# One MoE kernel on one core: the two experts of a pair in alternate blocks, and other start addresses for TensorE's stationary operands

## The chip, the cores and the metric

The kernel runs on one NeuronCore of a Trainium2 chip. The metric is the device time of one execution in microseconds, taken as the median over several runs. Lower is better. The profile is one further execution of the same program, recorded by the hardware profiler.

## The reference

The reference is a decoder of two blocks with 256 tokens and a model width of 1024, all in float32. The first block is two layers of mixer and feed-forward; its second feed-forward is the mixture of experts that this case is about:

```python
def moe_swiglu(h, router, w_gate, w_up, w_down):
    t = h.reshape(-1, d)                                  # 256 x 1024
    logits = (t @ router).astype(jnp.float32)
    top_v, top_i = lax.top_k(logits, TOP_K)               # TOP_K = 2 of N_EXPERTS = 8
    top_w = jax.nn.softmax(top_v, axis=-1)
    gates = jnp.sum(jax.nn.one_hot(top_i, N_EXPERTS) * top_w[..., None], axis=1)
    for e in range(N_EXPERTS):
        y_e = swiglu(t, w_gate[e], w_up[e], w_down[e])    # 1024 -> 3584 -> 1024
        out = out + gates[:, e:e + 1] * y_e
```

The second block (two layers of feed-forward, a mixer of convolutions and gating, feed-forward) follows; nothing in it is changed.

## The kernel before

**Precision.** TensorE takes float32 operands rounded to a shorter form (fp32r in the rows). To keep float32 accuracy each operand is split into a high and a low half, and a product is made of three matmuls: high x high, high x low, low x high (`mm3t`, lines 339 to 344 and their matmuls L341 to L343). Weights stream from HBM and are split on the way: a DMA brings 1 MB into one of four buffers `raw` (`load`, L297, on SP's queue), ScalarE (ACT) writes `hi` by a cast (L318), VectorE (DVE) writes `lo = raw - hi` (L319). One `hi` and one `lo` tile hold 128 x 1024 values, half a load; I call that a **part**. There are five `hi` and five `lo` buffers.

**The MoE** (`moe`, line 1059, and `moe_pass`, line 1219) works expert by expert. The experts are put into an order by their token counts: `ORDER` gives each of the eight positions a rank of size, and the positions whose rank is in `FEW = (1, 2, 3)`, the second of each of the first three pairs, are expected to hold at most `SMALL = 64` tokens. Such a **few** expert packs the high halves of its 64 tokens and the low halves of the same 64 into the 128 columns of one stationary operand, so it needs two matmuls (L1293, L1294) where a **full** expert (at most 128 tokens) needs three. It streams as many weights as a full one. A routing that doesn't fit the sizes goes through an extra pass under `tc.If` (L1205), which the inputs here don't take.

Two positions make a pair. `prep(p)` (line 1228) gathers the tokens of both experts of a pair by a selection matrix into `xeh` and `xel` (in every second pair into the model's own `xh` and `xl`), and makes the gates `gs` and the matrix `PT` that puts results back. Then, for each expert, the loop at line 1311 runs over seven blocks of 512 hidden columns:

1. gate and up: 8 parts, 4 for each of two PSUM banks, with the tokens (`xeh`) as the stationary operand and the weights moving;
2. SiLU and product into `mh` (full: L1330 on ACT, L1331 on DVE; few: two copies `mh` and `mu`, L1328 on ACT);
3. `down(*prev)` for the block before: 4 parts, stationary operand `mhh` (and `mhl`), into two PSUM banks `acc` that gather over all seven blocks;
4. transposes of `mh` (full L1352, few L1342 and then L1345, L1346), and the split into `mhh` and `mhl` (L478, L479).

So an expert has 84 parts. At its end `acc` is scaled and split into `yh`, `yl` (L1361, L1362), and `back()` multiplies by `PT` (16 matmuls, L1369, L1370) and adds to the model's state `X` (L401); it is called inside the first block of the next expert.

**PSUM.** All eight banks are taken: four buffers `bank` for gate and up, two `side0` and two `side1` for the rest (`acc`, the transposes, `prep`, `back`).

**Order of the work.** A scheduler places the instructions of each engine in a fixed queue, from its own estimate of when each is ready; every engine then works through its queue in order. Weight loads and splits are put ahead by `tc.high_priority`.

**Addresses.** Pools lay tiles one after the other. `SHIFT` pads the tile `Pf` (line 1230) and so moves the tiles behind it in their pool; lines 29 to 37 hold such constants. In the program before, the stationary tiles of a partition begin at these byte addresses modulo 512: `xeh`, `xel` at 288, `mhh`, `mhl` at 96, `xh`, `xl` in the MoE at 128.

Of the kernel before, what the change touches and what calls it, by code (L numbers as in the profile page):

```python
# [27 lines left out]
SMALL = 64  # L28
# [5 lines left out]
PHASE = {"h": 64, "l": 320}  # L34
STILL = 128
BASE = 128
SHIFT = 40

# [182 lines left out]
class Builder:  # L221
# [837 lines left out]
    def moe(self, gain):  # L1059
        nc, tc = self.nc, self.tc  # L1060
        p0 = self.par0
        with tc.tile_pool(name="moe", bufs=1) as pl, tc.tile_pool(name="moew", bufs=2) as wk:
            f = lambda n, name: pl.tile([128] + list(n), F32, name=name)

            early = {}
            self.expert = [0]
            with tc.high_priority(offset=AHEAD):
                for i in range(PRE):
                    early[0, i] = self.load(*self.moe_load(0, i))
                for (e, i), tags, pool, bufs in EARLY:  # L1070
                    ap, kt, n = self.moe_load(e, i)
# [14 lines left out]
            nc.gpsimd.tensor_scalar(key, p0("iota")[:, 0:8], 1.0 / 16, None, op0=ALU.mult)  # L1086
            nc.gpsimd.memset(key[:, 0:1], -1000.0)

            iotas = f([2, SMALL], "iotas")
            nc.gpsimd.tensor_copy(iotas, p0("iota")[:, 0:SMALL].rearrange("p (o n) -> p o n", o=1)  # L1090
                                  .to_broadcast([128, 2, SMALL]))
            ident2 = f([SMALL], "ident2")
# [8 lines left out]
            bt = self.side()  # L1101
# [19 lines left out]
            mm = nc.tensor.matmul  # L1121
# [62 lines left out]
            ci, ei = f([2, 8], "ci"), f([2, 8], "ei")  # L1184
# [12 lines left out]
            args = (pl, wk, xnh, xnl, posq, G, iotas, ident2)  # L1197
            nxt = self.moe_pass(args, False, 0, 1, None, early, more=True)

            early = {(2, i): self.weights(*self.moe_load(2, i)) for i in range(SPL)}  # L1200
            with tc.high_priority(offset=AHEAD):
                for i in range(SPL, SPL + PRE):
                    early[2, i] = self.load(*self.moe_load(2, i))
# [15 lines left out]
    def moe_pass(self, args, off, p0, p1, gain, early, cur=None, more=False):  # L1219

        nc = self.nc
        pl, wk, xnh, xnl, pos, G, iotas, ident2 = args
        mm = nc.tensor.matmul
# [1 line left out]
        ot = pl if off else wk  # L1225
        few = lambda e: ORDER[e] in FEW and not off

        def prep(p):

            Pf = wk.tile([128, 512 + SHIFT], F32, name="Pf", bufs=1)[:, :512] \  # L1230
                .rearrange("p (m a n) -> p m a n", m=2, a=2)
            Pr = wk.tile([128, 2, 256], F32R, name="Pr", bufs=1)
            for m in range(2):
                for a in range(2):
                    nc.vector.tensor_scalar(Pf[:, m, a], iotas.rearrange("p a n -> p (a n)") if few(2 * p + a) else iota,
                                            pos[:, m, 2 * p + a:2 * p + a + 1], None, op0=ALU.is_equal)
            nc.scalar.copy(Pr, Pf.rearrange("p m a n -> p m (a n)"))
            if p % 2 and not off:
                xeh, xel = self.xh, self.xl
            else:  # L1240
                xeh, xel = (pl.tile([128, KD, 256], F32R, name=n) for n in ("xeh", "xel"))
            for k in range(0, KD, 2):
                for src, dst, eng in ((xnh, xeh, nc.scalar.copy), (xnl, xel, nc.vector.tensor_copy)):
                    b = self.side()
                    for i in range(2):
                        for m in range(2):
                            mm(b[:, i * 256:(i + 1) * 256], src[:, m, (k + i) * 128:(k + i + 1) * 128], Pr[:, m],
                               start=(i == 0 and m == 0), stop=(i == 1 and m == 1), skip_group_check=True)
# [8 lines left out]
            bg = self.side()  # L1257
            for a in range(2):
                for m in range(2):
                    mm(bg[:, a * 9:(a + 1) * 9], Pf[:, m, a], G[:, m], start=(a == 0 and m == 0),  # L1260
                       stop=(a == 1 and m == 1), skip_group_check=True)
            gs = ot.tile([128, 2, 2], F32, name="gs")
            for a in range(2):
                e = 2 * p + a
                nc.vector.tensor_copy(gs[:, a, 0:1], bg[:, a * 9 + e:a * 9 + e + 1])
                nc.vector.tensor_copy(gs[:, a, 1:2], bg[:, a * 9 + 8:a * 9 + 9])
            bt = self.side()
            for a in range(2):
                for m in range(2):
                    nc.tensor.transpose(bt[:, a * 256 + m * 128:a * 256 + (m + 1) * 128], Pf[:, m, a], self.ident)  # L1270
            PT = ot.tile([128, 2, 256], F32R, name="PT")
            nc.scalar.copy(PT.rearrange("p a t -> p (a t)"), bt)
            return PT, gs, xeh, xel

        nxt, back = None, None
        for e in range(2 * p0, 2 * p1):
            a = e % 2
            if cur is None:
                if back:
                    back()  # L1280
                    back = None
                cur = prep(e // 2)
# [12 lines left out]

            def down(f0, hh, hl):
                if not acc:
                    acc.extend(self.side() for _ in range(2))
                for k0 in (0, 2):
                    wt = self.weights(wd.block(f0 + k0 * 128, 2, 0, D), 2, D)  # L1300
                    for k in range(2):
                        for n in range(2):
                            mms(acc[n], hh[:, k0 + k], None if hl is None else hl[:, k0 + k],
                                *wt(k, n * 512, (n + 1) * 512),
                                start=(f0 + k0 + k == 0), stop=(f0 + (k0 + k + 1) * 128 == 3584))

            prev = None
            for ci in range(7):
                b2 = []
                for wi in range(2):  # L1310
                    b = self.bank()
                    for ki in range(2):
                        i = ci * 4 + wi * 2 + ki
                        pre = early.get((e, i))
                        wt = pre if callable(pre) else self.weights(*self.moe_load(e, i), pre)
                        for k in range(4):
                            k0 = ki * 4 + k
# [14 lines left out]
                if ci == 6 and a == 1 and not off and (e + 1 < 2 * p1 or more):  # L1332
                    nxt = prep(e // 2 + 1)
                if prev:
                    down(*prev)
                bt = self.side()
                hh = wk.tile([128, 4, 128], F32R, name="mhh")
                if few(e):
                    n = 4 * SMALL
# [10 lines left out]
                else:  # L1350
# [5 lines left out]
                prev = (ci * 512, hh, hl)  # L1356
            down(*prev)
            yh, yl = wk.tile([128, D], F32R, name="yh", bufs=1), wk.tile([128, D], F32R, name="yl", bufs=1)
            for n in range(2):
                ns = slice(n * 512, (n + 1) * 512)  # L1360
                nc.scalar.activation(yh[:, ns], acc[n], AF.Copy, scale=gs[:, a, 0:1])  # L1361
                nc.vector.scalar_tensor_tensor(yl[:, ns], acc[n], gs[:, a, 0:1], yh[:, ns], ALU.mult, ALU.subtract)  # L1362

            def back(e=e, a=a, PT=PT, yh=yh, yl=yl):
                self.acc_open()
                for d in range(KD):
                    o = self.acc[d // 2][:, (d % 2) * T:(d % 2 + 1) * T]
                    ds = slice(d * 128, (d + 1) * 128)
                    mm(o, yh[:, ds], PT[:, a], start=(d % 2 == 0), stop=False, skip_group_check=True)  # L1369
                    mm(o, yl[:, ds], PT[:, a], start=False, stop=(d % 2 == 1), skip_group_check=True)  # L1370
                self.acc_close(1.0, gain if e == 7 else None)

            if a == 1:
                cur, nxt = nxt, None
        back()
        return cur

# [229 lines left out]
```

## Time and profile before

| | us |
|---|---|
| runs of the kernel before | 2446.11, 2459.65, 2447.5; median 2447.5 |
| profiled execution, device time | 2440.45 |
| its span, first to last instruction | 2438.7 |
| MoE, first gate matmul to the last evacuation of `acc` | 499 to 1495 |
| busy in the span: PE, DVE, ACT | 2350.8, 1872.1, 1434.3 |
| granted TensorE clock, mean | 0.991 |

The profiled execution is 7.05 us below the median of the runs; differences are worked out on the profiled one and carried over. A time window is given in microseconds from the start of the span. A matmul's recorded duration overlaps with the next one's, so TensorE's pace is read from the starts of successive matmuls. "Idle before" is the time an engine sat waiting before an instruction, and the arrow names what ended it.

### The profile page before, as it was taken

What the parts mean: (1) busy time and instruction counts of PE and PEld (TensorE: products, weight loads), DVE (VectorE), ACT (ScalarE), POOL (GpSimd) and SP (SyncE); (2) the same over time, 40 slices, a digit from 0 to 9 for tenths busy, and PEclk for the clock granted to TensorE, in tenths of its full rate; (3) what the DMA queues carried; (4) which work ended last, traced back from release to release, by engine and by line L of the source; (5) the groups of instructions that cost most, each with busy time, mean ns of one, the idle gap of its engine ahead of it and who ended that gap; (6) DMA issues with size and microseconds to landing.
All of it is one profiled execution on the core that took longest, in us unless ns stands there. A gap on an engine that the chain in (4) does not pass through costs nothing. (4 is left out here: it accounts for less than half of the span.)

```text
span 2438.7 us, 39247 instructions
## 1 busy us (share of the span) xinstructions
PE 2350.8 (96%) x15510; PEld 2092.3 (86%) x15510; DVE 1872.1 (77%) x2577; ACT 1434.3 (59%) x1803; POOL 21.9 (1%) x61
## 2 busy tenths in 40 slices
PE   7999999999898999999999999999999999999999
PEld 7899999787667776776777778999899999998998
DVE  8765796788888899888998888657865675587655
ACT  7544572477787778767877776445144454443444
POOL 0000000000000000000000000000000000000000
PEclk9999999999999999999999999999999999999999
DMA  6456442477998999999999997554455555545552
GB/s 227 146 189 207 165 153 72 173 287 293 334 353 330 342 352 389 351 347 353 382 350 356 347 350 287 199 184 154 138 214 206 190 176 196 175 137 188 180 204 87
DMA packets 91424, 595.24 MB, mean 244 GB/s; under 512 B 15776, under 2 KB 17184, under 8 KB 22240
## 3 DMA queue, kind: packets, MB, share of 16 engines
q1 hardware_dynamic: 90576, 590.52, 66.7%
q8 instruction: 123, 2.02, 0.3%
q0 software_dynamic: 368, 1.88, 0.2%
q14 instruction: 69, 0.57, 0.1%
q10 hardware_dynamic: 288, 0.26, 0.0%
HBM read 591.18 MB, written 1.44 MB: 243 GB/s over the span
## 5 line engine op out<-in xcount | busy, mean ns | idle before, releaser
L319 DVE TENSOR_TENSOR lo<-raw,hi 128x1024 fp32r<-128x1024 f32 (+1 forms) x1077 | 1272.1, 1217 | 359.0 <-ACT hi L318 354.9
L318 ACT CAST hi<-raw 128x1024 fp32r<-128x1024 f32 (+1 forms) x1077 | 1082.3, 1045 | 537.8 <-PE bank L336 232.4
L335 PE MATMUL bank<-xh,hi 128*128 128x256 f32 x2152 | 599.8, 279 | 15.4 <-ACT hi L318 10.9
L336 PE MATMUL bank<-xl,hi 128*128 128x256 f32 x2152 | 599.7, 279 | 0.4 <-DVE xl L412 0.2
L337 PE MATMUL bank<-xh,lo 128*128 128x256 f32 x2152 | 598.2, 278 | 0.0
L335 PEld LDWEIGHTS bank<-xh,hi 128*128 128x128 f32 x2152 | 405.4, 189 | 16.8 <-ACT hi L318 10.9
L337 PEld LDWEIGHTS bank<-xh,lo 128*128 128x128 f32 x2152 | 406.7, 189 | 0.7 <-DVE lo L319 0.4
L336 PEld LDWEIGHTS bank<-xl,hi 128*128 128x128 f32 x2152 | 405.7, 189 | 1.4 <-DVE xl L412 1.2
L336 PE MATMUL side<-hl,hi 128*128 128x256 f32 x880 | 244.0, 277 | 0.0
L337 PE MATMUL side<-hh,lo 128*128 128x256 f32 x880 | 244.0, 277 | 0.0
L335 PE MATMUL side<-hh,hi 128*128 128x256 f32 x880 | 243.8, 277 | 0.0
L342 PE MATMUL bank<-lo,xh 128*128 128x512 f32 (+1 forms) x432 | 167.7, 388 | 5.9 <-DVE lo L319 5.4
L341 PE MATMUL bank<-hi,xh 128*128 128x512 f32 (+1 forms) x432 | 165.2, 382 | 4.3 <-PEq L1205 4.3
L337 PEld LDWEIGHTS side<-hh,lo 128*128 128x128 f32 x880 | 166.0, 189 | 0.0
L335 PEld LDWEIGHTS side<-hh,hi 128*128 128x128 f32 x880 | 165.2, 188 | 0.0
L336 PEld LDWEIGHTS side<-hl,hi 128*128 128x128 f32 x880 | 165.2, 188 | 0.0
L343 PE MATMUL bank<-hi,xl 128*128 128x512 f32 (+1 forms) x432 | 164.7, 381 | 0.0
L342 PE MATMUL side<-lo,mhh 128*128 128x512 f32 x280 | 112.8, 403 | 0.4
L343 PE MATMUL side<-hi,mhl 128*128 128x512 f32 x280 | 110.4, 395 | 2.1 <-DVE mhl L479 2.1
L342 PEld LDWEIGHTS bank<-lo,xh 128*128 128x128 f32 x432 | 81.8, 189 | 32.7 <-DVE lo L319 18.6
L1294 PE MATMUL bank<-lo,xeh 128*128 128x512 f32 x224 | 95.6, 427 | 10.2 <-DVE lo L319 9.9
L341 PEld LDWEIGHTS bank<-hi,xh 128*128 128x128 f32 x432 | 81.8, 189 | 19.9 <-issue 4.5
(469 smaller groups left out, 3236.7 us busy)
## 6 DMA issues: line engine op xcount, KB each, us to landing
raw<-in_o_moe_w_down_dram SPq DMA_DIRECT2D x112, 1024.0 KB, 6.7
raw<-in_o_moe_w_gate_dram SPq DMA_DIRECT2D x110, 1024.0 KB, 6.7
raw<-in_o_moe_w_up_dram SPq DMA_DIRECT2D x110, 1024.0 KB, 6.7
raw<-in_ffn_w_gate_dram SPq DMA_DIRECT2D x44, 1024.0 KB, 4.9
raw<-in_ffn_w_up_dram SPq DMA_DIRECT2D x44, 1024.0 KB, 4.9
raw<-in_ffn_w_down_dram SPq DMA_DIRECT2D x44, 1024.0 KB, 4.9
raw<-in_o_w_in_dram SPq DMA_DIRECT2D x16, 1024.0 KB, 4.9
raw<-in_w_in_dram SPq DMA_DIRECT2D x20, 768.0 KB, 4.3
```

Source lines behind the costliest of these rows:

```text
L318: nc.scalar.copy(hi[:, :w], src)
L319: nc.vector.tensor_tensor(lo[:, :w], src, hi[:, :w], ALU.subtract)
L335: nc.tensor.matmul(out, wh, xh, start=start, stop=False, skip_group_check=True)
L336: nc.tensor.matmul(out, wh, xl, start=False, stop=False, skip_group_check=True)
L337: nc.tensor.matmul(out, wl, xh, start=False, stop=stop, skip_group_check=True)
L341: nc.tensor.matmul(out, xh, wh, start=start, stop=False, skip_group_check=True)
L342: nc.tensor.matmul(out, xh, wl, start=False, stop=False, skip_group_check=True)
L343: nc.tensor.matmul(out, xl, wh, start=False, stop=stop, skip_group_check=True)
L1294: mm(out, xh, wl, start=False, stop=stop, skip_group_check=True)
```

## The change

The loop over experts becomes a loop over pairs, and inside it blocks alternate: block 0 of the first expert, block 0 of the second, block 1 of the first, and so on. `down(*prev)` then belongs to the other expert's block. Both experts' sums are open at once, in all four `side` buffers; the transposes and `prep` therefore move to the `bank` buffers. The first expert is evacuated after its last down product, its `back` is called at the pair's end into `bank` buffers; the second expert's `back` is called as before, inside the next pair. The prefetch before the `tc.If` alternates too. Two paddings move start addresses.

```diff
-SHIFT = 40
+SHIFT = 24
...
-            iotas = f([2, SMALL], "iotas")
+            iotas = f([2 * SMALL + 24], "iotas")[:, 0:2 * SMALL].rearrange("p (a n) -> p a n", a=2)
...
-            early = {(2, i): self.weights(*self.moe_load(2, i)) for i in range(SPL)}
+            order = [(2, i) for i in range(4)] + [(3, i) for i in range(4)]
+            early = {x: self.weights(*self.moe_load(*x)) for x in order[:SPL]}
...
-        def prep(p):
+        def prep(p, new=self.bank):
...
-                    b = self.side()
+                    b = new()
...
-        for e in range(2 * p0, 2 * p1):
-            a = e % 2
+        for p in range(p0, p1):
...
-            wd = self.weight("o_moe_w_down", self.expert[e])
-            es = slice(a * 128, (a + 1) * 128)
-            acc = []
+            wds = [self.weight("o_moe_w_down", self.expert[2 * p + a]) for a in range(2)]
+            accs = [[], []]
...
-            def down(f0, hh, hl):
-                if not acc:
-                    acc.extend(self.side() for _ in range(2))
+            def down(a, f0, hh, hl):
+                if not accs[a]:
+                    accs[a].extend(self.side() for _ in range(2))
...
+            def end(a):
+
+                yh, yl = wk.tile([128, D], F32R, name="yh", bufs=1), wk.tile([128, D], F32R, name="yl", bufs=1)
...
-            prev = None
-            for ci in range(7):
+            prev, first = None, None
+            for ci, a in [(ci, a) for ci in range(7) for a in range(2)]:
...
                 if prev:
                     down(*prev)
-                bt = self.side()
+                if ci == 6 and a == 1:
+                    first = end(0)
+                bt = self.bank()
...
             down(*prev)
...
-            if a == 1:
-                cur, nxt = nxt, None
+            first(self.bank)
+            back = end(1)
+            cur, nxt = nxt, None
```

After the change the stationary tiles begin at these addresses modulo 512: `xeh`, `xel` at 384, `mhh`, `mhl` at 128, `xh`, `xl` in the MoE at 128 as before; all are 128 modulo 256.

What the scheduler makes of it shows first in ACT's queue. In the second pair before, a full expert's blocks (first piece) come in a row, and then a few expert's (second piece):

```order
L1330 ACTIVATE mh<-bank,gs 128x512
L318 CAST hi<-raw 128x1024 x6
L478 CAST mhh<-side_17318 128x512
L318 CAST hi<-raw 128x1024 x6
L1330 ACTIVATE mh<-bank,gs 128x512
```

```order
L1328 ACTIVATE mh<-bank,gs 128x512
L318 CAST hi<-raw 128x1024 x4
L1328 ACTIVATE mu<-bank,gs 128x512
L318 CAST hi<-raw 128x1024 x2
L1345 ACTIVATE mh<-side_17885 128x256
L318 CAST hi<-raw 128x1024 x2
L478 CAST mhh<-mh 128x4x64
L318 CAST hi<-raw 128x1024 x4
```

The same pair after the change, one turn of full and few block:

```order
L1351 ACTIVATE mh<-bank,gs 128x512
L318 CAST hi<-raw 128x1024 x6
L478 CAST mhh<-bank 128x512
L318 CAST hi<-raw 128x1024 x6
L1349 ACTIVATE mh<-bank,gs 128x512
L318 CAST hi<-raw 128x1024 x4
L1349 ACTIVATE mu<-bank,gs 128x512
L318 CAST hi<-raw 128x1024 x2
L1368 ACTIVATE mh<-bank 128x256
L318 CAST hi<-raw 128x1024 x2
L478 CAST mhh<-mh 128x4x64
L318 CAST hi<-raw 128x1024 x4
```

The full block's and the few block's instructions now alternate, and the number of `hi` casts between two instructions that wait for TensorE (4 or 6 in all) is what it was.

On SP's queue, at the start of the MoE, the loads of the second expert need its number, which SP reads (L1195). Before, and after:

```order
L1076 DMA rlo<-in_o_moe_w_up_dram 128x1024 x2
L1076 DMA ryh<-in_o_moe_w_gate_dram 128x1024
L1076 DMA ryl<-in_o_moe_w_gate_dram 128x1024
L297 DMA raw<-in_o_moe_w_gate_dram 128x2048
L1195 TENSOR_LOAD num
L1195 ISA x2
```

```order
L1076 DMA rlo<-in_o_moe_w_up_dram 128x1024 x2
L1076 DMA ryh<-in_o_moe_w_gate_dram 128x1024
L1076 DMA ryl<-in_o_moe_w_gate_dram 128x1024
L1195 TENSOR_LOAD num
L297 ISA
L297 DMA raw<-in_o_moe_w_gate_dram 128x2048
```

Before, the fifth and sixth load of gate weights go out ahead of the first read of a number; now the fifth load stands behind that read, and of the other reads, which came in one row of seven before the seventh load, five stand in a row behind the tenth.

On PE's queue the end of the last pair moved. Before, all of `back` (L1369, L1370) stands behind the last down product; after, the first expert's `back` into `bank` (L1321, L1322) stands between the second expert's last down products:

```order
L342 MATMUL side_21870<-lo,mhh 128x512
L343 MATMUL side_21870<-hi,mhl 128x512
L342 MATMUL side_21871<-lo,mhh 128x512
L343 MATMUL side_21871<-hi,mhl 128x512
L1369 MATMUL side_22705<-PT,yh 128x256
L1369 MATMUL side_22706<-PT,yh 128x256
L1370 MATMUL side_22705<-PT,yl 128x256
```

```order
L342 MATMUL side_20964<-lo,mhh 128x512
L343 MATMUL side_20964<-hi,mhl 128x512
L342 MATMUL side_20965<-lo,mhh 128x512
L343 MATMUL side_20965<-hi,mhl 128x512
L341 MATMUL side_20964<-hi,mhh 128x512
L341 MATMUL side_20965<-hi,mhh 128x512
L1321 MATMUL bank<-PT,yh 128x256
L1322 MATMUL bank<-PT,yl 128x256
```

What moved there are the first expert's 16 matmuls; the second expert's 16 still follow the last down product.

## Rows read from the trace of the kernel before

**Rows 1.** Busy time by window: the four pairs of experts, cut at the evacuations.
```profile
core 0: us, PE busy (x) PEld busy (x) DVE busy (x) ACT busy (x) POOL busy (x), PEclk, DMA share, GB/s
499.00:745.40 246.40, 232.31 (x1045) 180.72 (x1045) 213.34 (x220) 190.01 (x218) 0.00 (x0) 0.98 0.89 329
745.40:995.20 249.80, 235.56 (x1057) 181.08 (x1056) 221.20 (x228) 193.68 (x221) 0.00 (x0) 0.98 0.93 354
995.20:1241.80 246.60, 233.80 (x1060) 178.03 (x1058) 217.37 (x215) 189.25 (x219) 0.00 (x0) 1.00 0.95 357
1241.80:1494.90 253.10, 248.07 (x1094) 196.03 (x1095) 220.51 (x210) 181.88 (x201) 0.00 (x0) 1.00 0.93 349
```

**Rows 2.** Busy time by window: the three few experts (second half of pairs one to three).
```profile
630.00:745.40 115.40, 104.38 (x483) 79.12 (x482) 101.62 (x110) 91.42 (x113) 0.00 (x0) 0.96 0.97 357
...
877.10:995.20 118.10, 109.57 (x509) 80.55 (x508) 109.53 (x121) 99.94 (x120) 0.00 (x0) 0.99 0.97 376
...
1122.70:1241.80 119.10, 108.30 (x511) 79.85 (x509) 107.97 (x112) 98.24 (x119) 0.00 (x0) 1.00 0.97 369
```

**Rows 3.** Waits in the second pair's few expert (877.1 to 995.2): waiter, awaited, us, times, longest.
```profile
PEld bank L1294 <- DVE lo L319: 18.3, 35, 1.9
DVE lo L319 <- ACT hi L318: 6.4, 12, 1.3
...
ACT hi L318 <- DMA raw<-in_o_moe_w_down_dram: 3.2, 7, 0.8
ACT hi L318 <- DMA raw<-in_o_moe_w_up_dram: 3.0, 4, 1.4
```

**Rows 4.** ACT's timeline in the last pair: start us, us, instruction, idle before and releaser.
```profile
1400.40 0.59 ACT L478 CAST mhh<-side 128x512 fp32r<-128x512 f32 x1 [2.92 <-PE side L1352]
1400.88 3.90 ACT L318 CAST hi<-raw 128x1024 fp32r<-128x1024 f32 x4
1406.09 0.69 ACT L1330 ACTIVATE mh<-bank,gs 128x512 f32<-128x512 f32 x1 [1.31 <-PE bank L343]
1406.67 5.79 ACT L318 CAST hi<-raw 128x1024 fp32r<-128x1024 f32 x6
1415.56 0.59 ACT L478 CAST mhh<-side 128x512 fp32r<-128x512 f32 x1 [3.10 <-PE side L1352]
```

**Rows 5.** TensorE's weight loads just after, timeline.
```profile
1418.41 0.19 PEld L342 LDWEIGHTS bank<-lo,xh 128*128 128x128 f32 x1 [0.76 <-DVE lo L319]
```

**Rows 6.** PE's timeline, last pair: gate/up from xh, 12 matmuls apart; down from mhh, 6 apart.
```profile
1405.88 0.39 PE L341 MATMUL bank<-hi,xh 128*128 128x512 f32 x1
...
1408.61 0.39 PE L341 MATMUL bank<-hi,xh 128*128 128x512 f32 x1
...
1411.66 0.63 PE L341 MATMUL side<-hi,mhh 128*128 128x512 f32 x2
...
1413.06 0.63 PE L341 MATMUL side<-hi,mhh 128*128 128x512 f32 x2
```

**Rows 7.** PE's timeline, third pair: gate and up from xeh, 12 matmuls apart.
```profile
1033.08 0.39 PE L341 MATMUL bank<-hi,xeh 128*128 128x512 f32 x1
...
1035.88 0.40 PE L341 MATMUL bank<-hi,xeh 128*128 128x512 f32 x1
```

**Rows 8.** Busy time by window of 20 us: the slowest and the fastest DMA among few experts.
```profile
660.00:680.00 20.00, 18.97 (x88) 13.79 (x86) 16.38 (x17) 14.95 (x19) 0.00 (x0) 1.00 0.96 335
...
920.00:940.00 20.00, 18.44 (x79) 12.38 (x78) 18.91 (x20) 17.96 (x22) 0.00 (x0) 1.00 1.01 412
```

**Rows 9.** SP's timeline at the start of the MoE.
```profile
480.81 0.39 SPq L297 DMA_DIRECT2D raw<-in_o_moe_w_gate_dram  x1
503.58 2.99 SPq L297 DMA_DIRECT2D raw<-in_o_moe_w_up_dram  x2
```

**Rows 10.** PE's timeline at the end of the MoE.
```profile
1494.94 0.40 PE L343 MATMUL side<-hi,mhl 128*128 128x512 f32 x1
1495.65 0.50 PE L1369 MATMUL side<-PT,yh 128*128 128x256 f32 x2 [0.31 <-ACT yh L1361]
...
1498.07 0.28 PE L1370 MATMUL side<-PT,yl 128*128 128x256 f32 x1
```

More of the change, by code (lines that the diff above doesn't have):

```diff
@@ L1198, in moe @@
             nxt = self.moe_pass(args, False, 0, 1, None, early, more=True)
-            early = {(2, i): self.weights(*self.moe_load(2, i)) for i in range(SPL)}
+            order = [(2, i) for i in range(4)] + [(3, i) for i in range(4)]
+            early = {x: self.weights(*self.moe_load(*x)) for x in order[:SPL]}
             with tc.high_priority(offset=AHEAD):
-                for i in range(SPL, SPL + PRE):
-                    early[2, i] = self.load(*self.moe_load(2, i))
+                for x in order[SPL:SPL + PRE]:
+                    early[x] = self.load(*self.moe_load(*x))
             n = nc.values_load(cnti[0:1, 0:1], min_val=0, max_val=2 * T)
@@ L1256, in prep @@
                         eng(xeh[:, k:k + 2, 128 + SMALL:], b[:, :, 128 + SMALL:])
-            bg = self.side()
+            bg = new()
             for a in range(2):
@@ L1266, in prep @@
                 nc.vector.tensor_copy(gs[:, a, 1:2], bg[:, a * 9 + 8:a * 9 + 9])
-            bt = self.side()
+            bt = new()
             for a in range(2):
@@ L1281, in moe_pass @@
                     back = None
-                cur = prep(e // 2)
+                cur = prep(p)
             PT, gs, xeh, xel = cur
-            wd = self.weight("o_moe_w_down", self.expert[e])
-            es = slice(a * 128, (a + 1) * 128)
-            acc = []
+            wds = [self.weight("o_moe_w_down", self.expert[2 * p + a]) for a in range(2)]
+            accs = [[], []]
             def mms(out, xh, xl, wh, wl, start, stop):
@@ L1294, in mms, with back @@
                 mm(out, xh, wl, start=False, stop=stop, skip_group_check=True)
-            def down(f0, hh, hl):
-                if not acc:
-                    acc.extend(self.side() for _ in range(2))
+            def down(a, f0, hh, hl):
+                if not accs[a]:
+                    accs[a].extend(self.side() for _ in range(2))
                 for k0 in (0, 2):
-                    wt = self.weights(wd.block(f0 + k0 * 128, 2, 0, D), 2, D)
+                    wt = self.weights(wds[a].block(f0 + k0 * 128, 2, 0, D), 2, D)
                     for k in range(2):
                         for n in range(2):
-                            mms(acc[n], hh[:, k0 + k], None if hl is None else hl[:, k0 + k],
+                            mms(accs[a][n], hh[:, k0 + k], None if hl is None else hl[:, k0 + k],
                                 *wt(k, n * 512, (n + 1) * 512),
                                 start=(f0 + k0 + k == 0), stop=(f0 + (k0 + k + 1) * 128 == 3584))
-            prev = None
-            for ci in range(7):
+            def end(a):
+                yh, yl = wk.tile([128, D], F32R, name="yh", bufs=1), wk.tile([128, D], F32R, name="yl", bufs=1)
+                for n in range(2):
+                    ns = slice(n * 512, (n + 1) * 512)
+                    nc.scalar.activation(yh[:, ns], accs[a][n], AF.Copy, scale=gs[:, a, 0:1])
+                    nc.vector.scalar_tensor_tensor(yl[:, ns], accs[a][n], gs[:, a, 0:1], yh[:, ns], ALU.mult,
+                                                   ALU.subtract)
+                def back(new=None, PT=PT, last=(2 * p + a == 7)):
+                    self.acc_open(new)
+                    for d in range(KD):
+                        o = self.acc[d // 2][:, (d % 2) * T:(d % 2 + 1) * T]
+                        ds = slice(d * 128, (d + 1) * 128)
+                        mm(o, yh[:, ds], PT[:, a], start=(d % 2 == 0), stop=False, skip_group_check=True)
+                        mm(o, yl[:, ds], PT[:, a], start=False, stop=(d % 2 == 1), skip_group_check=True)
+                    self.acc_close(1.0, gain if last else None)
+                return back
+            prev, first = None, None
+            for ci, a in [(ci, a) for ci in range(7) for a in range(2)]:
+                e = 2 * p + a
+                es = slice(a * 128, (a + 1) * 128)
                 b2 = []
@@ L1331, in moe_pass @@
                     nc.vector.scalar_tensor_tensor(h, b2[1], gs[:, a, 1:2], h, ALU.mult, ALU.mult)
-                if ci == 6 and a == 1 and not off and (e + 1 < 2 * p1 or more):
-                    nxt = prep(e // 2 + 1)
+                if ci == 6 and a == 1 and not off and (p + 1 < p1 or more):
+                    nxt = prep(p + 1)
                 if prev:
                     down(*prev)
-                bt = self.side()
+                if ci == 6 and a == 1:
+                    first = end(0)
+                bt = self.bank()
                 hh = wk.tile([128, 4, 128], F32R, name="mhh")
@@ L1355, in moe_pass @@
                     self.split(fl(hh), fl(hl), bt)
-                prev = (ci * 512, hh, hl)
+                prev = (a, ci * 512, hh, hl)
             down(*prev)
[L1358 to L1371, printed above, removed]
-            if a == 1:
-                cur, nxt = nxt, None
+            first(self.bank)
+            back = end(1)
+            cur, nxt = nxt, None
         back()
```

## The prediction

> **What bounds the kernel now.** The change touches the MoE alone, so I read the busy time by window, first for the four pairs of experts [rows 1]. Pairs one to three hold a full and a few expert each and take 246.4, 249.8 and 246.6 us, 742.8 in all; the last holds two full ones and takes 253.1. No engine is full over a pair: DVE is busy 213.3 to 221.2 us of some 247, ACT less, the DMA engines 0.89 to 0.95 of the time. PE's busy time doesn't tell its pace, because records of successive matmuls overlap. Together the four pairs are 996 us of the 2438.7 of the span.
>
> The same view for the few experts alone [rows 2] shows what a pair's mean hides. They take 115.4, 118.1 and 119.1 us, and DVE is busy in 0.881, 0.927 and 0.907 of that, 0.905 on the mean. A part costs DVE one subtraction whether the expert is few or full; TensorE does four matmuls on it in a few expert and six in a full one. The list of waits in a few expert says the same [rows 3]: TensorE's weight loads wait 18.3 us for `lo`, DVE waits 6.4 us for `hi`, ACT 6.2 us for two kinds of weights from HBM. So DVE sets the pace there, with the DMA close behind. The few expert runs short of split weights while the full one next to it leaves DVE idle.
>
> In a full expert TensorE sets the pace, but not without holes. ACT's timeline in the last pair [rows 4] shows the mechanism. ACT works its queue in order: after six `hi` casts it stands before the cast of `mhh` and waits 3.10 us for TensorE's transposes, although a weight buffer may be free. When TensorE has finished the parts that were cast ahead, its weight load waits 0.76 us for `lo` [rows 5]. The queue order, not the number of buffers, limits how far weights are split ahead.
>
> **The change part by part.** A pair's instructions are the same before and after: 168 parts, 168 `hi`, 168 `lo`, the same transposes, 2 x 16 `back` matmuls, one `prep`. What moves is the order.
>
> *Alternating blocks, pairs one to three.* DVE's work of 213.3 + 221.2 + 217.4 = 651.9 us [rows 1] stays. The floor of the three pairs is that sum, 652 instead of 742.8. The other end is no gain, 742.8, if every wait of ACT's queue stays. Between them I take the row in which DVE already sets the pace with this kind of queue, the few experts: DVE busy 0.905 of the time. 651.9 / 0.905 = 720. That is **22.5 us less**. I take this and not the floor because the queue order printed ahead shows that ACT still meets an instruction that waits for TensorE after every two to six casts, as in a few expert now; I take it and not the upper end because the full block's slack, in which DVE can get ahead by the two parts that the queue allows, now comes after every few block and not once in a pair.
>
> *DMA.* The bytes don't change: 329 x 246.4 + 354 x 249.8 + 357 x 246.6 [rows 1] make 257.5 MB. At 720 us they need 358 GB/s; the few experts got 357, 376 and 369, 367 on the mean [rows 2], at which the three pairs take 702. So the DMA doesn't set the end of my sum, but it is only 18 us under it, and it makes 702 a likelier lower end than DVE's 652.
>
> The Trainium skill ("DMA: Bandwidth & Descriptors", Specifications) gives a limit from HBM of about 358 GB/s for each core, where both cores of a pair stream; by it the three pairs could not come under 257.5 / 0.358 = 719 us, an estimate by that page, and all that lies below my forecast would fall away. Here one core runs, and the trace shows more: 376 GB/s over a whole few expert [rows 2] and 412 over 20 us [rows 8]; the measurement decides, and the range keeps the lower values.
>
> *Start addresses.* Twelve successive matmuls take 2.73 us with `xh` as the stationary operand, which begins at 128 modulo 256, so 227.5 ns each; six take 1.40 us with `mhh`, at 96, so 233.3 [rows 6]; with `xeh`, at 288, twelve take 2.80, again 233.3 [rows 7]. So the pace goes with the start address, by 5.8 ns a matmul, as far as these rows can separate it from the tile. After the change all three stand at 128 modulo 256. In the last pair TensorE sets the pace and 2 x 168 down matmuls gain: 336 x 5.8 ns = **2 us**. In pairs one to three I count nothing, since DVE sets the pace; if it didn't, the full experts' 168 x 3 down matmuls and 336 x 2 gate and up matmuls would give 6.8 us more. Below: 0, if the pace has another cause.
>
> *PSUM.* The transposes and `prep` now share four `bank` buffers with gate and up: three in use in a block, one more than before. A new gate bank waits for the bank of the last transposes, which must be split anyway before the next down product. I cost it at nothing; the cover is that one spare buffer, and if it is gone, each of 42 blocks waits for one split, some 0.6 us, as the `mhh` cast [rows 4], 25 us in all. That is the worst of the bounds and not likely, because the split is queued ahead of the next bank's evacuation.
>
> *Ends.* The first expert's `back` moves from inside the second expert to the pair's end. By PE's queue its 16 matmuls stand among the last down products, so they fill a place and add none. The second expert's evacuation must wait until `yh` is free: at most a whole `back`, 2.4 us (1495.65 to 1498.07, [rows 10]), at the two places where no next block follows, the end of pair one and of pair four. Between 0 and 4.8 I take **1 us**, near the lower end, as the queue shows most of those matmuls ahead of the last down products.
>
> *SP's queue.* The second expert's first load now waits for a number that SP reads. Before, the next load after those reads goes out at 503.58, 22.8 us after the one before them [rows 9]; now only one read of seven stands ahead of it, so it goes out no later, and TensorE has eight parts of 1.4 us each to work on. Five reads stand behind the tenth load: at most a few us once, between 0 and 5. I take 0, as a `raw` buffer is not free earlier anyway.
>
> **Sum**: -22.5 - 2 + 1 = -23.5. The profiled execution's 2440.45 becomes 2417; the median of the runs stands 7.05 higher, so the forecast is **2424**. A measurement of this kernel can tell some 0.5% from no change, 12 us: below 2435.3 it is faster, above 2459.7 slower.
>
> **The rivals.**
>
> *The averaging is better than in a few expert, and the DMA sets the end.* For it: over two blocks TensorE's and DVE's needs are nearly equal, so that DVE needs less lead than in a few expert alone; DVE's floor is 652. At the few experts' mean of 367 GB/s the three pairs take 702, at the best one's 376 685. The sum is 41 to 58 less, with the two small terms 2406 to 2389. Against it: the waits of ACT's queue. Chance 0.20.
>
> *The queue order gives back what the alternation brings.* ACT's casts between two waits for TensorE are as many as before, so the split weights may never be more than two parts ahead when a few block begins, and two parts, 2.8 us of a full block, don't cover a few block's deficit. Then each turn takes as long as a full and a few block one after the other, and the three pairs stay at 743: only -2 + 1 remain, 2446. For it: ACT's waits of 2.92 and 3.10 us [rows 4] lie in full blocks, which now stand beside few ones. Against it: after such a wait the few block finds at least those two parts each time, where a few block now follows another one. Chance 0.25.
>
> *Slower: the DMA can't keep the rate through the alternation.* Now a few expert drains four `raw` buffers for 118 us and a full one lets them fill. If alternating blocks got no more than the slowest 20 us among the few experts, 335 GB/s [rows 8], the three pairs would take 257.5 / 0.335 = 769, 26 more: 2473. It decides from a rate below 257.5 / 742.8 = 347 GB/s over pairs one to three. For it: the DMA share of 0.96 in that same window. Against it: 354 and 357 GB/s as the means of whole pairs already [rows 1]. Chance 0.07. With the worst of the PSUM term, which would also end near 2449 to 2472, the slower side has 0.09.
>
> **How the numbers follow.** Forecast 0.46, first rival 0.20, second 0.25, slower 0.09. The range goes from 2395, inside the first rival, to 2452, above the second one: it leaves out the slower cases and the far end of the first rival. The forecast with its own error of some 10 us lies almost all under 2435, the first rival wholly, so faster has 0.63; the second rival and the rest of the forecast make the same 0.28; slower 0.09.
>
> **What would show it.** In the new profile pairs one to three should take about 240 us each, with DVE busy in 0.90 of the time and 358 GB/s, and no stretch of 100 us in which TensorE's loads wait 18 us for `lo`. If the first rival holds, they take 229 to 234 and ACT's waits for DMA grow; if the second, 247, with ACT waiting for transposes and banks as now. Six down matmuls should start 1.365 us apart, and twelve from `xeh` 2.73; if they stay at 1.40 and 2.80, the address isn't the cause. The last pair should take some 251. The prediction is wrong if pairs one to three together move by less than 10 us or by more than 45, or if time moves outside the MoE.

## The result and the profile after

The change made the kernel slower: 2469.68 us (median of 12 runs, 2459.59 to 2476.37) against 2445.29 (12 runs, 2429.43 to 2459.65), a ratio of 1.0099, 95% interval 1.0076 to 1.0123. The forecast of 2424 and its range, up to 2452, both missed. The profiled execution of the changed kernel took 2469.37 us, its span is 2467.6.

Busy time of the engines in the page of the changed kernel, for the whole span:

```profile
PE 2363.2 (96%) x15510; PEld 2105.3 (85%) x15510; DVE 1875.4 (76%) x2577; ACT 1434.6 (58%) x1803; POOL 21.8 (1%) x61
```

The work is the same (DVE 1872.1 before), so 29 us more of span are waiting or a slower pace. The next view is the busy time by window in the changed kernel, the four pairs cut at the second expert's last evacuation, which answers to [rows 1]:

```profile
507.25:758.88 251.63, 234.56 (x1043) 180.35 (x1041) 214.32 (x219) 190.80 (x220) 0.00 (x0) 0.97 0.87 332
758.88:1017.93 259.05, 239.86 (x1075) 183.52 (x1075) 224.71 (x232) 195.26 (x226) 0.00 (x0) 0.98 0.92 345
1017.93:1268.22 250.29, 235.34 (x1058) 179.60 (x1057) 219.20 (x217) 190.89 (x221) 0.00 (x0) 0.99 0.93 352
1268.22:1520.10 251.88, 243.69 (x1082) 195.02 (x1080) 216.80 (x205) 179.84 (x199) 0.00 (x0) 0.99 0.91 345
```

Pairs one to three were to fall from 743 to 720; they take 761. The last pair is 1.2 us shorter. To compare kernels I use one stretch throughout, **the MoE time**: from the first gate matmul to the first new `xh`. Their rows in the changed kernel (PE's and ACT's timeline):

```profile
507.25 0.47 PE L341 MATMUL bank<-hi,xeh 128*128 128x512 f32 x1
...
1526.14 1.71 ACT L411 ACTIVATE xh<-X,p 128x256 fp32r<-128x256 f32 x4 [4.42 <-DVE X L401]
```

That is 1018.9 us; in the kernel before it was 998.6:

```profile
499.40 0.48 PE L341 MATMUL bank<-hi,xeh 128*128 128x512 f32 x1
...
1497.95 1.71 ACT L411 ACTIVATE xh<-X,p 128x256 fp32r<-128x256 f32 x4
```

So 20.3 us of the loss are in the MoE. The MoE began 7.85 us later in this execution; TensorE's order ahead of it is unchanged, and the executions of the kernel before alone lie 30 us apart.

**A turn in the middle of a pair.** DVE makes one product `mh` per block, so its starts are a clock of the blocks. In the changed kernel's second pair, five turns (a full and a few block each) lie between these two of six such rows:

```profile
807.96 0.75 DVE L1352 SCALAR_TENSOR_TENSOR mh<-bank,gs,mh 128x512 f32<-128x512 f32 x1 [1.42 <-PE bank L343]
...
976.06 0.74 DVE L1352 SCALAR_TENSOR_TENSOR mh<-bank,gs,mh 128x512 f32<-128x512 f32 x1
```

168.1 / 5 = 33.6 us. In the kernel before, four full blocks and four few blocks of the same pair lie between these:

```profile
796.25 0.74 DVE L1331 SCALAR_TENSOR_TENSOR mh<-bank,gs,mh 128x512 f32<-128x512 f32 x1
...
866.00 0.74 DVE L1331 SCALAR_TENSOR_TENSOR mh<-bank,gs,mh 128x512 f32<-128x512 f32 x1
...
905.28 0.41 DVE L1346 TENSOR_TENSOR mh<-mh,side 128x256 f32<-128x256 f32 x1
...
969.38 0.41 DVE L1346 TENSOR_TENSOR mh<-mh,side 128x256 f32<-128x256 f32 x1
```

17.4 and 16.0, together 33.5. (Third pair, read likewise: 33.8 after, 34.8 before.) Alternation leaves the pace of the middle where it was, within 1 us a turn. Yet from the first product of pair one to the first of pair four it is 738.8 us before (first two rows) and 757.9 after (last two), 19.0 more:

```profile
517.33 0.75 DVE L1331 SCALAR_TENSOR_TENSOR mh<-bank,gs,mh 128x512 f32<-128x512 f32 x1
1256.16 0.75 DVE L1331 SCALAR_TENSOR_TENSOR mh<-bank,gs,mh 128x512 f32<-128x512 f32 x1
...
521.59 0.74 DVE L1352 SCALAR_TENSOR_TENSOR mh<-bank,gs,mh 128x512 f32<-128x512 f32 x1
1279.46 0.74 DVE L1352 SCALAR_TENSOR_TENSOR mh<-bank,gs,mh 128x512 f32<-128x512 f32 x1
```

So the loss lies at the pairs' beginnings and ends. There, PE's timeline of the changed kernel shows these waits, behind the first product, where the second pair ends and the third begins, and at the end of the MoE:

```profile
522.39 1.11 PE L1375 MATMUL bank<-p,mh 128*128 128x128 f32 x4 [3.97 <-DVE mh L1352]
...
1004.80 0.50 PE L341 MATMUL bank<-hi,xeh 128*128 128x512 f32 x1 [1.01 <-DVE X L401]
1008.24 0.79 PE L342 MATMUL bank<-lo,xeh 128*128 128x512 f32 x1 [2.94 <-DVE lo L319]
...
1029.38 0.39 PE L1322 MATMUL side<-PT,yl 128*128 128x256 f32 x1 [3.06 <-DVE yl L1313]
...
1518.37 0.50 PE L1321 MATMUL side<-PT,yh 128*128 128x256 f32 x2 [0.33 <-ACT yh L1312]
1524.37 0.58 PE L1322 MATMUL side<-PT,yl 128*128 128x256 f32 x1 [5.50 <-DVE yl L1313]
```

The last two answer to [rows 10]; from the first product with `yh` to the first with `yl` it is 6.00 us here, and in the kernel before it was 0.78 (1495.65 to this row):

```profile
1496.43 0.39 PE L1370 MATMUL side<-PT,yl 128*128 128x256 f32 x1 [0.28 <-DVE yl L1362]
```

After such a wait TensorE runs slowly for a while: from 520 to 540 the granted clock was 0.83, the lower of its two levels (1.2 GHz) for part of that time.

### The profile page after: what moved, and what is told of

Same layout as the page of the kernel before. It is cut to its first block, busy times and chain, and to the rows that moved or that the text cites. A ratio compares the mean times of both kernels' runs of the same rounds, so it can differ in the third digit from the quotient of the medians.

```text
span 2467.6 us, 39307 instructions
## 1 busy us (share of the span) xinstructions
PE 2363.2 (96%) x15510; PEld 2105.3 (85%) x15510; DVE 1875.4 (76%) x2577; ACT 1434.6 (58%) x1803; POOL 21.8 (1%) x61
## 4 chain that ended last, share of the span: by engine, by line
PE 49%; DVE 11%; DMA 5%; ACT 3%; issue 2%; DVEq 0%; ACTq 0%
PE bank L336 6%; PE bank L337 6%; PE bank L335 6%; DVE lo L319 5%; PE bank L342 4%; PE bank L343 4%; PE bank L341 3%; PE side L336 3%; PE side L335 3%; DVE av L1465 3%; PE side L337 3%; ACT hi L318 2%; DMA raw<-in_o_moe_w_down_dram 2%; PE side L341 2%; PE side L342 1%
```

## The experiments

Fourteen kernels. The ratio is to the kernel before on the same chip; the MoE time is from each one's profiled execution. Six kernels leave loads, waits or results out and were executed once.

| run | ratio, 95% interval | MoE us |
|---|---|---|
| before | 1 | 998.6 |
| the change | 1.0099, 1.0076 to 1.0123 | 1018.9 |
| e1 addresses alone | 0.9977, 0.9956 to 0.9998 | 990.7 |
| e2 addresses, all in `bank` | 1.0065, 1.0043 to 1.0087 | 1009.1 |
| e5 addresses, prep in `bank` | 1.0004, 0.9975 to 1.0033 | 998.1 |
| e9 as e2, first blocks in `side` | 0.9984, 0.9957 to 1.0010 | 993.4 |
| e3 change, first way back in `side` | 1.0130, 1.0100 to 1.0160 | 1018.9 |
| e6 change, one block ahead | 1.0101, 1.0065 to 1.0137 | 1020.0 |
| e10 change, first block in `side` | 1.0062, 1.0038 to 1.0085 | 1008.9 |
| e12 as e10, two more edits | 1.0069, 1.0048 to 1.0090 | 1012.5 |
| e13 as e10, no first way back | one execution | 1002.4 |
| e14 as e9, no first way back | one execution | 991.7 |
| e4 change, fewer loads | one execution | 993.7 |
| e7 change, no waits for products | one execution | 996.2 |
| e8 change, both | one execution | 953.3 |
| e11 as e1, fewer loads | one execution | 1020.9 |

A MoE time is one execution. Where there is a ratio, the difference to the kernel before that it gives (the ratio's excess over 1, times the median before) stands 1.3 to 5.3 us from that of the MoE times, in e3 11.4. So a difference of some 5 us between two MoE times is not clear of the spread.

**A ladder from before to the change: e1, e2.**

```diff
# e1, on the kernel before: the diff's two paddings, nothing else
# e2, on e1:
-        b = self.side()        (prep: also bg and bt)
+        b = self.bank()
-                bt = self.side()
+                bt = self.bank()
```

> The kernel before with the two paddings alone; the order of the blocks and PSUM as before. If the forecast's address term is right (5.8 ns a matmul, worth something only where TensorE sets the pace), it is 2 us faster than before, out of the last pair. Rival: TensorE sets the pace in the full experts of all pairs too, and the full block's period falls there from 17.9 to about 17.5 us; then 8.8 us faster (2 + 6.8). Third: the addresses cost time and hold part of the 24 us that the change lost; then it is slower than before by 5 us or more.

> The run before with, in addition, the transposes and the gather of the next pair in the four bank buffers, experts still one after the other. Theory (the loss belongs to the order of the work at the pairs' ends): within 3 us of the run with the addresses alone. Rival (the shared PSUM buffers cost what the forecast had as its worst bound): up to 25 us slower than that run, with waits of gate and up for a bank in every block.

The paddings alone gain 7.9 us of MoE time (5.6 by the ratio). The banks then cost 18.4, with the experts still one after the other; alternation adds another 9.8 (by the ratios some 21 and 8). So my theory, that the loss belongs to the alternation's lump at the pairs' ends, was wrong for two thirds of it: the shared PSUM buffers cost it.

**Which use of `bank`: e5, e9.**

```diff
# e5, on e1: prep in bank, transposes stay in side
# e9, on e2:
-                bt = self.bank()
+                bt = self.side() if ci == 0 else self.bank()
```

> The kernel before with the paddings, and of the PSUM part only the gather for the next pair (prep) in the four bank buffers; transposes stay in side. The run with both in bank was 0.9 per cent, some 21 us, slower than the paddings alone, all of it at the three pair ends. Theory A (prep's ten bank buffers, taken in turn with gate and up, hold the pair's end): nearly the whole 21 us come with it, 2449 or more against a before of 2437. Theory B (the transposes' buffers in the first blocks of a pair do it): within 4 us of the paddings alone, about 2430.

> The run with addresses and all of prep and the transposes in bank, experts one after the other, but the first block of each expert transposes in side. In that first block no down product of a block before lies between gate and up and the transposes, and with the transposes in bank TensorE's queue has no gate and up of the next block ahead of them (0 in place of 22). Theory A (this is where the transposes in bank cost, TensorE waits 3 to 4 us there and runs on at the lower clock): the time falls from 1.0065 of before to that of the gather alone in bank, 1.000 to 1.002. Rival (transposes in bank cost a little in each block): it stays at 1.005 or more.

e5 fell between its theories: prep in `bank` costs 7.4 us in e5; e9, which has it too, lies only 2.7 over e1, so its price is not clear of the spread. Theory A of e9 held, with a ratio a little under its range: with only each expert's first block back in `side`, 15.7 of the 18.4 us are gone. Why there: in every later block `down(*prev)` stands between gate and up and the transposes and gives ACT and DVE time to make `mh`. A first block has no such product ahead. In the kernel before, the printed order has 33 matmuls of the second block's gate and up in front of the first block's transposes (the expectation's 22 leaves out one of the three lines); with the transposes in `bank` there are none, and TensorE waits. The first transposes of the MoE before, without a wait, and in e2, with the matmuls behind them; then the window behind them in e2 and in e9:

```profile
518.40 0.60 PE L1352 MATMUL side<-p,mh 128*128 128x128 f32 x4
```

```profile
520.37 1.12 PE L1352 MATMUL bank<-p,mh 128*128 128x128 f32 x4 [3.97 <-DVE mh L1331]
...
522.57 0.63 PE L341 MATMUL bank<-hi,xeh 128*128 128x512 f32 x1
523.00 0.63 PE L342 MATMUL bank<-lo,xeh 128*128 128x512 f32 x1
```

```profile
520.00:540.00 20.00, 19.63 (x77) 16.12 (x78) 13.75 (x14) 12.65 (x13) 0.00 (x0) 0.84 0.75 275
```

```profile
520.00:540.00 20.00, 20.00 (x92) 16.54 (x91) 18.65 (x18) 16.06 (x17) 0.00 (x0) 1.00 0.99 374
```

In e2 TensorE waits 3.97 us, then runs at a mean clock of 0.84 and makes 77 recorded matmuls in 20 us instead of 92; DVE is busy 13.75 instead of 18.65 us, and the DMA brings 275 GB/s instead of 374. e2 keeps SP's old queue order, so this stall, which the change has too (522.39, above), isn't SP's number read.

**The same cure in the change, and what is left: e10, e3, e6, e12.**

```diff
# e10, on the change:
-                bt = self.bank()
+                bt = self.side() if ci == a == 0 else self.bank()
# e3, on the change: two side buffers in turn, X added after each
-            down(*prev)
-            first(self.bank)
+            first(True)
+            down(*prev)
# e6, on the change; first's way back and prep use two side buffers, the prefetch follows the order
-            for ci, a in [(ci, a) for ci in range(7) for a in range(2)]:
+            for ci, a in [(0, 0)] + [x for i in range(6) for x in ((i + 1, 0), (i, 1))] + [(6, 1)]:
# e12, on e10: the order of e6 in pair four alone, and around yh, yl:
+                    with self.tc.high_priority(offset=FIRST):
```

> The changed kernel, but the first block of each pair transposes in side (16 more gate and up matmuls then stand ahead of these transposes in TensorE's queue). Theory A: the 4.0 us wait for the first product at the start of pair one and the slow clock behind it go, there and less at the other pair starts: 8 to 14 us less than the change, 1.004 to 1.007 of before. Rival (the first pair starts late for another reason, SP's queue or the loads): less than 4 us.

> The changed kernel, but the first expert's way back goes through the two side buffers that its own sum has just freed, two at a time, and is called ahead of the last down product instead of behind it in all four bank buffers. Theory (the lump at the pair's end costs the time: X additions ahead of the few expert's product on VectorE, gate matmuls that wait for a bank, then the lower clock): 3 to 5 us less in each of four pairs, 2469.7 becomes about 2455. Rival (the loss comes with the alternation itself, in every turn): no change over 3 us.

> The changed kernel with the first expert one block ahead of the second, so that its sum is complete and its two side buffers are free before the pair's last block; its way back and prep go through these two, the transposes stay in bank. Theory A (the loss is the lump of prep and way back in bank at the pairs' ends, the alternation itself is neutral): the pairs' ends come back to those of before, and the time to that of the paddings alone, 0.997 to 1.000 of before, some 25 us under the change. Rival (alternation or the transposes' buffers cost): it stays above 1.005. Turns in the middle of a pair stay at 33.6 us by both.

> The changed kernel with the first block of each pair transposing in side (as in the run before last), and two further edits: yh and yl are placed ahead in the queues (at two pair starts the back product waited 3.1 us for yl behind subtractions, and ran on at the lower clock), and in the last pair the first expert runs one block ahead, so that its way back no longer lies in front of the last evacuation (there the last back product waited 5.5 us for yl). Theory (these named waits are what alternation itself loses): the MoE, from the first gate matmul to the first new xh, falls from 1008.9 us to 993 to 998, level with the sequential order with the same banks (993.4), and the run comes to 0.998 to 1.002 of before. Rival (alternation loses more at the pairs' ends than the waits that were named): above 1.004, MoE over 1003.

e10 did what its theory said: 10.0 us less. (By the trace 40 matmuls more stand ahead of the first transposes there, 32 of gate and up and the 8 transposes of the few block, not 16; TensorE's wait falls from 3.97 to 1.34 us.) The theories of e3 and e6 failed: other buffers for the first way back, or a shift by one block, gained nothing. e12 took away the waits it named (the last back product now waits 0.28 us for `yl`, not 5.50), and the MoE did not get shorter. So taking away single waits at a pair's end gained nothing here. One that was there in the change (1008.24, above) stands in e12 as it did:

```profile
1004.34 0.80 PE L342 MATMUL bank<-lo,xeh 128*128 128x512 f32 x1 [2.94 <-DVE lo L319]
```

**Is it the first expert's way back? e13, e14.**

```diff
# e13, on e10:
-            first(self.bank)
# e14, on e9:
+            if a == 0:
+                back = None
```

> The changed kernel with the first block of each pair transposing in side, and the way back of each pair's first expert left out (4 x 16 matmuls and 4 x 4 additions to X; its results are missing in the output). Its MoE, first gate matmul to first new xh, was 1008.9 us with the way back. Theory C (the way back of the first expert, put into the pair's end, is what alternation loses against the sequential order): 20 to 25 us less, 985 to 990. Rival (the ends of two experts lying together cost, whatever is in them): no more than in the sequential order, 4 to 10 us less, 999 to 1005.

> The same left out of the sequential order with the same banks (addresses, prep and transposes in bank, first block of each expert in side), whose MoE took 993.4 us. Both theories: 4 to 10 us less, 983 to 989, since 16 matmuls take 1.9 us at 117 ns and there are four experts. The difference to the run beside it is the price of the way back in the alternation.

Without it the alternating order gets 6.5 us shorter, the sequential one 1.8 (less than the 4 I expected at least). So moving this way back into the pair's end costs about 4.7 us, which single executions don't tell from nothing; 10.7 remain between e13 and e14, as e13's rival had it. Theory C, with 20 to 25 us, is out. Which step at the two experts' joint end costs the 10.7 was not found.

**What holds a turn at 33.6 us: e4, e7, e8, e11.**

```diff
# e4, on the change: few experts, blocks 1 to 6
+                        if ci and few(e):
+                            if wi == 0:
+                                kept[ki] = self.load(*self.moe_load(e, i))
+                            pre = kept[ki]
# e7, on the change (and so in all seven operations on products)
-                    nc.scalar.activation(h, b2[0], AF.Silu, scale=gs[:, a, 1:2])
+                    nc.scalar.activation(h, still, AF.Silu, scale=gs[:, a, 1:2])
# e8: both.  e11: e4's edit on e1
```

> The changed kernel, but in blocks 1 to 6 of the few experts the up product uses the gate weights that are already in raw: casts, subtractions and matmuls as before, 2 of 12 loads of a turn left out. Theory (ACT's queue order holds a turn, which stands at 33.6 us as a full and a few block one after the other did): a turn stays within 0.7 us of 33.6, at a DMA share near 0.81. Rival (the DMA, busy 0.97 of a turn at 372 GB/s, is the floor): the turn follows the bytes, 10 of 12, and falls to 28 to 31 us.

> The changed kernel, but the seven operations on the products (silu, copies, products, split) read a constant tile in SBUF in place of the PSUM banks: same counts and sizes, results of gate, up and transposes unread, so that ACT and DVE never stand in their queues for TensorE's products. Theory (the queue order holds a turn): a turn falls from 33.6 to 31 us or less, near TensorE's own 30. Rival (the DMA holds it, 12.6 MB at the 372 GB/s of such a turn): it stays above 33.

> The two edits together: constant input for the operations on the products, and up products of the few experts from gate's raw weights (2 of 12 loads of a turn left out). Theory (queue order alone): as without the fewer loads, 31 or less. Rival (DMA alone): as with the fewer loads alone, 32.5. If both hold a turn in part: near TensorE's 30, and well under each edit alone.

> The kernel before with the paddings, blocks one expert after the other, and in blocks 1 to 6 of the few experts the up product from gate's raw weights (4 of 12 loads in a full plus a few block are the few block's gate and up; 2 are left out here). Theory (before, the few experts ran at the DMA's rate, 384 to 399 GB/s, not at VectorE's): a few block falls from 16.0 us to 14.5 or less, that is TensorE's and VectorE's own need. Rival (VectorE and the queue order set a few block, as the prediction had it): it stays within 0.4 us of 16.0. Full blocks stay at 17.8 by both.

Busy time by window, middle of pair two: the change (five turns), e4 (five), e7 (three), e8 (four), each cut at products of one expert:

```profile
807.96:976.06 168.10, 161.51 (x703) 119.85 (x702) 149.28 (x140) 131.82 (x150) 0.00 (x0) 1.00 0.97 372
```

```profile
792.91:955.29 162.38, 156.58 (x701) 120.59 (x700) 148.43 (x140) 131.89 (x150) 0.00 (x0) 1.00 0.83 321
```

```profile
829.04:932.52 103.48, 96.85 (x421) 71.64 (x420) 89.75 (x85) 80.82 (x91) 0.00 (x0) 1.00 0.97 367
```

```profile
825.50:948.47 122.97, 121.15 (x560) 97.49 (x560) 118.18 (x113) 105.95 (x121) 0.00 (x0) 1.00 0.89 340
```

A turn takes 33.6, 32.5, 34.5 and 30.7 us. Waits taken away alone: no gain, the DMA is at 0.97. Loads taken away alone: only 1.1 us, though the DMA has slack at 0.83; the queues hold it then. Both: 30.7, and TensorE is busy almost without a gap (121.15 of 122.97). So two limits stand within 1.1 us of each other, the DMA first, and TensorE's own pace some 2 us under both. The edit of e4 also holds `raw` for two casts, which can lengthen its turn; in e8 the same edit let a turn take 30.7. e11 told nothing on the few experts alone: in pair two a few block took 16.8 us and the MoE 1020.9, 30 us more than in e1, as `raw` was held for two casts, and in its few blocks TensorE waited for copies of `mh` on ACT at a clock of 0.89.

e7 also says something on the pairs' ends. Its turns are no shorter than the change's, yet its MoE takes 996.2 us, 22.7 less. So most of what the change loses outside the middle turns goes when ACT and DVE no longer wait for gate, up and transposes; the stall that e10 cured, 10.0 us, may be part of it. This is one execution, and which of these waits cost the rest is not shown.

## Why the prediction was wrong

- **"Alternating blocks, pairs one to three": 22.5 us less.** This step failed. It took DVE's share of 0.905 over whole few experts [rows 2] as what the queues allow in a turn, and counted the rest of 742.8 as recoverable. But 742.8 / 21 = 35.4 us is not a turn; a turn in the middle took 33.5 to 34.8 already, and the rest lay at the pairs' ends, which alternation does not remove. Pairs one to three took 761 us, 18 more instead of 22.5 less; a turn stayed at 33.6, held by the DMA and, 1.1 us under it, by the queues (e4, e7, e8). In the middle of a few expert before, the DMA stood at its end:

```profile
905.30:986.90 81.60, 77.79 (x365) 56.86 (x364) 76.13 (x88) 71.36 (x87) 0.00 (x0) 1.00 0.99 389
```

  DVE 0.93, DMA 0.99, 389 GB/s. I had the 412 of [rows 8] and the mean of 367, and called the DMA no limit at 720; as a mean over a pair that is so, in the middle of a pair it isn't. The Trainium skill ("DMA: Bandwidth & Descriptors", Specifications) gives about 358 GB/s for each core where both stream; this row and the 372 of the alternating turns are above it, so its figure wasn't the limit here.
- **"PSUM": costed at nothing, 25 us as the worst bound, "not likely".** This step failed by 18.4 us. The size of the bound was right and its place wrong: no wait in each of 42 blocks, but one lost overlap in the first block of an expert, 15.7 of the 18.4. I looked at whether a buffer was free, not at what TensorE's queue has ahead of the transposes when there is no down product. The printed order would have told it.
- **"Ends": 1 us, at most 4.8.** Alternation added 9.8 (e2 to the change), 15.5 with the first blocks cured (e9 to e10). The way back is at most some 5 of it; the rest is open, and e7 points to ACT's and DVE's waits for products.
- **"Start addresses": 2 us.** The pace was right. Twelve matmuls from `xeh` now take 2.72 us, three down matmuls 0.68, in PE's timeline of the changed kernel:

```profile
1015.41 0.39 PE L341 MATMUL bank<-hi,xeh 128*128 128x512 f32 x1
...
1018.13 0.39 PE L341 MATMUL bank<-hi,xeh 128*128 128x512 f32 x1
...
1455.27 0.40 PE L341 MATMUL side<-hi,mhh 128*128 128x512 f32 x1
1455.95 0.39 PE L341 MATMUL side<-hi,mhh 128*128 128x512 f32 x1
```

  [rows 6, 7] had 2.80 and, for six, 1.40. e1 gained 5.6 by the ratio and 7.9 of MoE time; its interval, 0.5 to 10.7, holds both the 2 and the 8.8 with the full experts of pairs one to three counted. From the second to the last product, a full block of pairs one and three was 0.33 and 0.28 us shorter than before, where 72 matmuls at 5.8 ns would give 0.42; in pair two, where only the 24 down matmuls have a new address, it was 0.12 for 0.14. So TensorE sets the pace in full blocks there too, for the most part. The last pair, forecast 2 us shorter, is 1.2.
- **"SP's queue": 0.** Nothing speaks against it: e2 has the old order of loads and the same stall.
- **The rivals.** The second one had the length of a turn: as long as a full and a few block one after the other. Its reason, the queues' waits, is one of the two limits and not the first: without those waits a turn took 34.5 us (e7). And it gave 2446, since it too costed the banks and the ends at nothing. The slower one named 2473, near the result, by luck: the rate over pairs one to three, 343 GB/s, is under its 347, but in the turns the DMA gave 372; where pairs begin and end it was busy less (0.80, at 315 GB/s, from 520 to 540).

The lowest ratio among the kernels that leave nothing out is that of e1, the paddings without the alternation: 2428.27 us against 2436.62 on its chip.

## What to carry to other kernels

Before a mean over a stage is called slack, cut the stage into its steady part and its ends: a change of the steady order can only win what the steady part loses. When a tile moves to another PSUM pool, look at the first block, where the usual cover is missing, and at what each queue then has ahead of it. Put a part of a change that stands by itself, as the paddings here, to its own run.

## What had not been expected of the hardware

One wait of 3.97 us in TensorE cost more than itself: matmuls from `xeh` were 0.43 us apart behind it, for 0.23 else, and the mean clock over 20 us was 0.84. In alternating turns the DMA engines were busy 0.97 of the time at 372 GB/s; in few experts alone, at 0.99, they moved 389. Why the same share moves less there was not tried.
